# A smaller descriptor scratch, three more chunk places, and 17 chunks loaded ahead in the expert stage

## The chip, the cores and the metric

One core of one Trainium2 chip runs the program. The metric is the device time of one execution in microseconds. Three executions of the kernel before took 1064.9, 1062.97 and 1060.87 us; the median, 1062.97, is what the change is compared with.

## The reference

An encoder trunk of two layers works on 512 tokens of width 1024 in float32. Cut to what matters:

```python
h = layer_norm(x, ln0_g, ln0_b)
for i in range(DEPTH):
    u = h @ w_in[i]
    mix = concat([hyena(u), diff_attention(u), pool(u)]) @ w_out[i]
    h = layer_norm(DN_ALPHA * h + mix, ln1_g[i], ln1_b[i])
    y_moe = hier_moe(h, ...)     # top-1 group of 4, top-2 of its 4 experts; silu(h w1) * (h w3) @ w2
    y_ple = sigmoid(h @ ple_wg[i] + ple_bg[i]) * (p[i] @ ple_wp[i])
    h = layer_norm(DN_ALPHA * h + y_moe + y_ple, ln2_g[i], ln2_b[i])
return h
```

The kernel reads the weights of all 16 experts (three matrices of 1 MB each) from HBM once per layer.

## The kernel before, in words

All large weights come as a stream of units, 139 per layer. A unit is one chunk of weights (128 partitions of 4 KB, that is 512 KB) with the matmuls that use it. `pump` (from L233) handles the stream: SP issues the chunk's DMAs into a tile `raw` (L240), and `split` (L222 to L225) makes two tiles of it, `whi` by a cast on ACT (L224) and `wlo` by a subtraction on DVE (L225). PE then multiplies with three matmuls per product, hi by hi, hi by lo and lo by hi (`mm3`, L218 to L220). `pump` is called when a unit begins, with two depths: up to `ahead_raw` units further the loads are issued, and up to `ahead_split` units further the splits. The depths are pairs of numbers by stage, `P_A` (5, 3), `P_LN` (14, 1), `P_MOE` (14, 3, set in `layer` when the route is through), `P_END` (7, 3, from expert `E_END`, the tenth) and `P_LAST` (8, 4, in the last expert).

All tiles of 4 KB per partition are drawn from one pool by `s4` (L197): `raw`, `whi`, `wlo`, the stream `h`, the transposed tokens `xT`, the experts' outputs `ye`, the gate's `plz`, the attention's `prob` and so on. The pool has `NSLOT` places (L153), 33 before. A new tile waits for the last user of the tile whose place it takes; which that is comes out when the program is built. So the number of places and the depths together set which transfer, cast or subtraction waits for which.

The order of one layer: input projection, three head groups and output projection; LN1 (`gains` of LN1 are loaded at L293); the router (`route`), whose count `rt_cnt` is read by every engine at L1343 and decides at L1344 whether a rarely used branch for overfull experts is run; the gate's first half (`pl` matmuls, `plz`); 16 experts; LN2. SP's queue is in order, so a chunk that stands behind L1343 on SP is loaded when the count has come. An expert's tokens are gathered by an indirect DMA of POOL (`xe`, L1251), transposed, multiplied by w1 and w3 (four `in` units, two 256 KB DMAs each) and by w2 (two `out` units, 512 KB each), and scatter-added to `yd` in HBM by an indirect DMA of POOL (L1257). The place of `ye` comes free when that scatter has landed. The outputs of the last two experts are kept in `yl` and added at the end.

POOL's DMAs write their descriptors to a scratch in each partition's memory, whose size is an argument where the program is made (L1685). Outside the stages named, the order of instructions is the scheduler's, which sees a tile's wait for its place as any other wait.

Of the kernel before, what the change touches and what calls it, by code (L numbers as in the profile page):

```python
# [136 lines left out]
def _view(t, shape):  # L137
    if len(shape) == 2:
        return t
    letters = "abcdef"[:len(shape) - 1]  # L140
    return t.rearrange(f"p ({' '.join(letters)}) -> p {' '.join(letters)}", **dict(zip(letters, shape[1:])))
# [8 lines left out]


class Trunk:
    NSLOT = 33  # L153
    NHALF = 6
    FSTEPS = (0, 7), (1, 5), (3, 5), (3, 8)
    P_A = 5, 3
# [16 lines left out]
    P_LAST = 8, 4  # L173
    P_END = 7, 3
    P_LN = 14, 1
    P_MOE = 14, 3
    APART = [[], [0, 1, 3]]
    ZPE = [[1], [1, 2, 3]]

# [17 lines left out]
    def s4(self, shape, name, dt=F32):  # L197
        n = int(np.prod(shape[1:]))
        return _view(self.slots.tile([128, n], dt, name=name, tag="s4", bufs=self.NSLOT,
                                     padded_shape=[128, SLOT]), shape)  # L200
# [1308 lines left out]
    def layer(self, i):  # L1509
# [99 lines left out]
        self.xe, self.xT, self.act, self.actT, self.yl, self.hotT, self.plz = {}, {}, {}, {}, {}, {}, {}  # L1609
        self.ahead_raw, self.ahead_split = self.P_MOE  # L1610
        for e in range(2):
# [87 lines left out]
```

## Time and profile before

| | before |
|---|---|
| median of three executions | 1062.97 us (1060.87 to 1064.9) |
| the profiled execution | 1060.65 us, span 1058.7 us, mean granted clock 0.974 |
| PE busy | 977.4 us, 92% of the span |
| DVE, ACT, POOL busy | 779.3, 613.5, 166.3 us |
| DMA | 197.49 MB, mean 187 GB/s |

The span runs from the first to the last instruction; the profiled execution's own time is 2 us longer. "Busy" is time with an instruction in work; an engine that waits for a tile is idle, and the profile names the engine and line, or the DMA, whose end released it. `SPq` is SP's queue, which only issues DMAs here. Names as `raw<-in_moe_w_dram` are a DMA's target and source.

### The profile page before, as it was taken

The numbers are of one execution on the slowest core, as the hardware profiler recorded it, in microseconds if no ns is written. First come the engines' busy times: TensorE is split into PE (matmuls) and PEld (weight loads), VectorE is DVE, ScalarE is ACT, GpSimd is POOL, SyncE is SP. The second block draws the span as 40 slices with busy tenths as digits, with TensorE's granted clock in tenths as the row PEclk, the third lists the DMA queues.
The fourth block names the chain that finished last, engine by engine and source line by source line (L and its number), as shares of the span: only waits on it lengthen the run. The fifth ranks groups of instructions, "written<-read, shape, count | busy, mean of one in ns | idle before, by whom it ended". The sixth has DMA issues, their size and how long they took to land. (4 is left out here: it accounts for less than half of the span.)

```text
span 1058.7 us, 14409 instructions
## 1 busy us (share of the span) xinstructions
PE 977.4 (92%) x4869; PEld 805.7 (76%) x4870; DVE 779.3 (74%) x1301; ACT 613.5 (58%) x1046; POOL 166.3 (16%) x170
## 2 busy tenths in 40 slices
PE   4999999999889898999999999999998989999895
PEld 3887889897767676777768889798776768877673
DVE  7576887767685676878885578847678677888776
ACT  5425464656552746887754246654645375887673
POOL 1101000000122112332121100000002222333112
PEclk9999999999999998999989999999999999999998
DMA  8815121231864988999994412122186498899974
GB/s 261 234 35 140 51 79 42 70 95 65 308 209 109 334 245 274 292 300 308 264 312 122 112 55 66 49 64 88 50 307 221 107 329 275 283 311 318 306 211 159
DMA packets 156010, 197.49 MB, mean 187 GB/s; under 512 B 20296, under 2 KB 123786, under 8 KB 155925
## 3 DMA queue, kind: packets, MB, share of 16 engines
q1 hardware_dynamic: 135253, 155.58, 44.8%
q0 software_dynamic: 20672, 40.87, 15.1%
q8 instruction: 42, 0.69, 0.3%
q14 instruction: 43, 0.35, 0.1%
HBM read 182.85 MB, written 29.36 MB: 200 GB/s over the span
## 5 line engine op out<-in xcount | busy, mean ns | idle before, releaser
L225 DVE TENSOR_TENSOR wlo<-raw,whi 128x1024 fp32r<-128x1024 f32 (+2 forms) x278 | 321.9, 1182 | 78.9 <-ACT whi L224 68.1
L224 ACT CAST whi<-raw 128x1024 fp32r<-128x1024 f32 (+2 forms) x278 | 275.0, 1025 | 42.1 <-DMA yd<-ye,rt_tok 11.0
L218 PE MATMUL e<-whi,xT 128*128 128x512 f32 x256 | 108.8, 425 | 3.5 <-ACT xT L224 1.8
L219 PE MATMUL e<-wlo,xT 128*128 128x512 f32 x256 | 106.0, 414 | 5.9 <-DVE wlo L225 5.9
L220 PE MATMUL e<-whi,xT 128*128 128x512 f32 x256 | 103.4, 404 | 0.0
L218 PE MATMUL pj<-whi,hT 128*128 128x384 f32 x256 | 89.8, 351 | 2.3 <-ACT hT L224 1.8
L219 PE MATMUL pj<-wlo,hT 128*128 128x384 f32 x256 | 88.0, 344 | 0.3 <-DVE wlo L225 0.3
L220 PE MATMUL pj<-whi,hT 128*128 128x384 f32 x256 | 87.2, 341 | 0.2
L1257 POOL DMA_INDIRECT yd<-ye,rt_tok x28 | 47.0, 1677 | 196.5 <-ACT ye L1322 115.5
L868 ACT ACTIVATE prob<-sc,mx 128x512 f32<-128x512 f32 x64 | 43.7, 687 | 38.9 <-DVE mx L867 37.8
L219 PEld LDWEIGHTS e<-wlo,xT 128*128 128x128 f32 x256 | 50.0, 195 | 20.8 <-DVE wlo L225 12.0
L1251 POOL DMA_INDIRECT xe<-hd,rt_tok x32 | 48.2, 1507 | 100.4 <-PE tr L376 55.8
L218 PEld LDWEIGHTS e<-whi,xT 128*128 128x128 f32 x256 | 50.0, 195 | 14.5 <-ACT whi L224 3.5
L308 POOL TENSOR_TENSOR ors<-rs_y,mhalf 128x4 f32<-128x4 f32 x8 | 8.5, 1057 | 333.8 <-DVE rs_y L307 333.8
L220 PEld LDWEIGHTS e<-whi,xT 128*128 128x128 f32 x256 | 49.6, 194 | 10.2
L218 PE MATMUL mo<-whi,YT 128*128 128x512 f32 x128 | 53.6, 419 | 0.2 <-ACT YT L224 0.2
L219 PE MATMUL e<-wlo,actT 128*128 128x512 f32 x128 | 52.4, 409 | 1.2 <-DVE wlo L225 1.2
L218 PEld LDWEIGHTS pj<-whi,hT 128*128 128x128 f32 x256 | 48.7, 190 | 4.8 <-ACT hT L224 2.5
L218 PE MATMUL e<-whi,actT 128*128 128x512 f32 x128 | 48.5, 403 | 3.7 <-ACT whi L224 2.8
L219 PE MATMUL pl<-wlo,hT 128*128 128x512 f32 x128 | 51.3, 401 | 0.5 <-DVE wlo L225 0.5
L218 PE MATMUL pl<-whi,hT 128*128 128x512 f32 x128 | 51.1, 405 | 0.4 <-ACT whi L224 0.4
L220 PE MATMUL pl<-whi,hT 128*128 128x512 f32 x128 | 51.3, 401 | 0.0
(340 smaller groups left out, 2317.0 us busy)
## 6 DMA issues: line engine op xcount, KB each, us to landing
raw<-in_moe_w_dram SPq DMA_DIRECT2D x256, 256.0 KB
raw<-in_moe_w_dram SPq DMA_DIRECT2D x64, 512.0 KB
raw<-in_w_in_dram SPq DMA_DIRECT2D x96, 128.0 KB
raw<-in_w_in_dram SPq DMA_DIRECT2D x16, 512.0 KB
raw<-in_ple_wg_dram SPq DMA_DIRECT2D x16, 512.0 KB
raw<-in_w_out_dram SPq DMA_DIRECT2D x14, 512.0 KB
tabi<-c_tabi_dram POOLq DMA_DIRECT2D x8, 516.0 KB, 4.9
tabf<-c_tabf_dram POOLq DMA_DIRECT2D x8, 512.0 KB, 5.5
```

The lines of the kernel that those rows point to most:

```text
L218: mm(ps, a[0], b[0], start=start, stop=False)
L219: mm(ps, a[0], b[1], start=False, stop=False)
L220: mm(ps, a[1], b[0], start=False, stop=stop)
L224: self.nc.scalar.copy(hi, src)
L225: self.nc.vector.tensor_sub(lo, src, hi.bitcast(F32))
L308: nc.gpsimd.tensor_tensor(out, y, self.mhalf[:, :n], op=OP.pow)
L868: nc.scalar.activation(p[:, c], o, AF.Exp, bias=mx[:, c:c + 1], accum_out=sm[:, c:c + 1])
L1251: self.nc.gpsimd.indirect_dma_start(out=x, out_offset=None, in_=self.hd[:, :], in_offset=bass.IndirectOffsetOnAxis(ap=tok, axis=0), bounds ...
L1257: self.nc.gpsimd.indirect_dma_start(out=self.yd[:, :], out_offset=bass.IndirectOffsetOnAxis(ap=row, axis=0), in_=y, in_offset=None, bounds ...
```

## The change

Three numbers change: the scratch for descriptors is set to 4 KB per partition where it was the default of 16 KB; the 12 KB become three places of 4 KB in the pool; and the depth of loads in the expert stage is 17 where it was 14.

```diff
-    NSLOT = 33
+    NSLOT = 36
...
-    P_MOE = 14, 3
+    P_MOE = 17, 3
...
-    nc = _bacc.Bacc("TRN2", target_bir_lowering=False, num_devices=1)
+    nc = _bacc.Bacc("TRN2", target_bir_lowering=False, num_devices=1, dynamic_dma_scratch_size=4096)
```

On SP, in layer 0, this is the order around the read of the count before the change (a `raw` of 128x2x256 is half an `in` unit, one of 128x1024 an `out` unit; `gb` are the router's bias vectors):

```order
L1584 DMA bg<-in_ple_bg_dram 128x1024
L240 DMA raw<-in_moe_w_dram 128x1024 x2
L240 DMA raw<-in_moe_w_dram 128x2x256 x6
L1017 DMA gb<-in_moe_bgc_dram 128x4
L1017 DMA gb<-in_moe_bgf_dram 128x16
L1343 TENSOR_LOAD rt_cnt
L1343 ISA x2
L240 DMA raw<-in_moe_w_dram 128x2x256 x2
L1344 COMPARE_AND_BRANCH
```

And with the change:

```order
L1584 DMA bg<-in_ple_bg_dram 128x1024
L240 DMA raw<-in_moe_w_dram 128x1024 x2
L240 DMA raw<-in_moe_w_dram 128x2x256 x8
L240 DMA raw<-in_moe_w_dram 128x1024
L1017 DMA gb<-in_moe_bgc_dram 128x4
L1017 DMA gb<-in_moe_bgf_dram 128x16
L240 DMA raw<-in_moe_w_dram 128x1024
L1343 TENSOR_LOAD rt_cnt
L1343 ISA x2
L240 DMA raw<-in_moe_w_dram 128x2x256 x2
L1344 COMPARE_AND_BRANCH
```

One `in` unit and two `out` units more stand ahead of the read of the count; in layer 1 the same three units move ahead of it.

On DVE, in the last block of the attention of layer 0, the order changes as follows (`prob` is the softmax product of L873, `mx` its row maximum, `aT` the transposed probabilities, `mo` the output projection's sum):

```order
-L872 TENSOR_SCALAR rsm<-rsm,nlam,smx 128x1
-L225 TENSOR_TENSOR wlo<-raw,whi 128x1024
-L873 SCALAR_TENSOR_TENSOR prob<-prob,rsm 128x512
+L964 SCALAR_TENSOR_TENSOR h<-h,mo 128x512
+L871 RECIPROCAL rsm<-smx 128x1
+L964 SCALAR_TENSOR_TENSOR h<-h,mo 128x512
+L872 TENSOR_SCALAR rsm<-rsm,nlam,smx 128x1
+L225 TENSOR_TENSOR aT<-at,aT 128x4x128
+L873 SCALAR_TENSOR_TENSOR prob<-prob,rsm 128x512
+L225 TENSOR_TENSOR wlo<-raw,whi 128x1024
```

The subtraction `wlo` comes behind the last `prob`, and a subtraction `aT` ahead of it.

On PE, in the route of layer 0 (`lgT` are the router's scores, L1100 the counting of ranks; `pl` are the gate's matmuls that fill its gaps):

```order
 L218 MATMUL pl<-whi,hT_104 128x512
+L219 MATMUL pl<-wlo,hT_104 128x512
+L220 MATMUL pl<-whi,hT_105 128x512
+L218 MATMUL pl<-whi,hT_104 128x512
 L1032 MATMUL lgT<-hT_105,gwhl 20x256 x2
```

Three matmuls of the gate stand ahead of the scores, and in the same way four ahead of L1100. In the expert stage PE, DVE, ACT and POOL keep their order; there only SP's differs, by the three units and by the gains of LN2 (L293), which come three units later.

## Rows read from the trace of the kernel before

**Rows 1.** Page, part 1: busy time and share of the span, each engine.

```profile
span 1058.7 us, 14409 instructions
PE 977.4 (92%) x4869; PEld 805.7 (76%) x4870; DVE 779.3 (74%) x1301; ACT 613.5 (58%) x1046; POOL 166.3 (16%) x170
```

**Rows 2.** Table by stretches: start and end, length, busy time per engine, clock, DMA.

```profile
core 0: us, PE busy (x) PEld busy (x) DVE busy (x) ACT busy (x) POOL busy (x), PEclk, DMA share, GB/s
312.00:322.00 10.00, 10.00 (x55) 7.96 (x53) 8.93 (x41) 1.37 (x3) 0.00 (x0) 1.00 0.03 6
810.00:826.00 16.00, 15.52 (x89) 12.25 (x88) 14.34 (x48) 6.79 (x10) 0.00 (x0) 1.00 0.32 114
842.00:880.00 38.00, 35.16 (x162) 28.08 (x162) 30.40 (x36) 28.59 (x41) 12.32 (x8) 0.96 1.00 298
```

**Rows 3.** Waits of SP's queue: 312:340, 810:842, 880:913, 913:1000, in this order (us, times, longest).

```profile
SPq L1343 <- DVE rt_cnt L1131: 9.3, 1, 9.3
SPq L1343 <- DVE rt_cnt L1131: 16.7, 1, 16.7
SPq L240 <- DMA yd<-ye,rt_tok: 11.8, 2, 7.0
SPq L240 <- DMA raw<-in_moe_w_dram: 25.4, 43, 2.0
```

**Rows 4.** Timeline of ACT, 974:996: start, duration, operation, idle before and its releaser.

```profile
980.34 1.04 ACT L224 CAST whi<-raw 128x1024 fp32r<-128x1024 f32 x1 [3.32 <-DMA raw<-in_moe_w_dram]
```

**Rows 5.** Timeline of PE, 978:992.

```profile
981.44 0.50 PE L218 MATMUL e<-whi,actT 128*128 128x512 f32 x1 [1.24 <-ACT whi L224]
982.70 0.50 PE L219 MATMUL e<-wlo,actT 128*128 128x512 f32 x1 [0.76 <-DVE wlo L225]
987.86 0.73 PE L218 MATMUL pl<-whi,hT 128*128 128x512 f32 x2 [0.44 <-ACT whi L224]
989.12 0.50 PE L219 MATMUL pl<-wlo,hT 128*128 128x512 f32 x1 [0.53 <-DVE wlo L225]
```

**Rows 6.** Table by stretches, two short ones of the expert stages.

```profile
417.00:424.00 7.00, 6.81 (x23) 5.55 (x24) 5.10 (x6) 4.34 (x7) 1.59 (x1) 0.55 0.56 146
983.00:987.00 4.00, 4.00 (x11) 2.73 (x10) 2.40 (x4) 1.57 (x3) 0.00 (x0) 0.57 0.82 270
```

**Rows 7.** Timeline of PE, 1015:1030.

```profile
1022.74 0.50 PE L219 MATMUL e<-wlo,xT 128*128 128x512 f32 x1 [0.76 <-DVE wlo L225]
1025.70 0.50 PE L219 MATMUL e<-wlo,xT 128*128 128x512 f32 x1 [1.31 <-DVE wlo L225]
```

**Rows 8.** Waits of PE, 480:540.

```profile
PE e L219 <- DVE wlo L225: 2.1, 5, 0.8
PE el L1430 <- ACT yl L1315: 1.6, 1, 1.6
```

**Rows 9.** Timelines of DVE, 262:270, and PE, 264:272.

```profile
265.56 1.22 DVE L225 TENSOR_TENSOR wlo<-raw,whi 128x1024 fp32r<-128x1024 f32 x1
266.69 0.75 DVE L873 SCALAR_TENSOR_TENSOR prob<-prob,rsm 128x512 f32<-128x512 f32 x1
267.58 0.63 PE L881 MATMUL at<-cst,prob 128*128 128x128 f32 x4 [2.03 <-DVE prob L873]
```

**Rows 10.** Page, part 5: one group of the gate's matmuls.

```profile
L219 PE MATMUL pl<-wlo,hT 128*128 128x512 f32 x128 | 51.3, 401 | 0.5 <-DVE wlo L225 0.5
```

**Rows 11.** Tile ye, 330:1040: scatters; who waited for them; issue to landing.

```profile
L1257 POOL DMA_INDIRECT yd<-ye,rt_tok x28: 1575/1591/2011, 361.2 to 1025.1; - x28
  ACT whi L224: 11.0, 4
  DVE wlo L225: 4.7, 2
DMA to landing us min/median/max: 6.1/8.8/10.5
```

**Rows 12.** Timeline of PE, 412:428.

```profile
417.19 0.69 PE L1292 MATMUL e<-cst,act 128*128 128x128 f32 x2 [4.68 <-DVE act L1275]
```

## The prediction

> **What bounds the kernel now.** The page's first section comes first: TensorE (PE) is busy for 977.4 of 1058.7 us, and no other engine for more than 779.3 [rows 1]. So time can only be won where PE stands idle, 81 us in all, or runs at half clock, and the question is how much of this the three chunks reach. The table by stretches [rows 2] shows where DMA does not carry: while the router works the DMA engines are nearly empty, at a share of 0.03 (312 to 322 us, layer 0) and 0.32 (810 to 826, layer 1). Right behind it they are full, 1.00 at 298 GB/s in 842 to 880. In the expert stage the chunks come at what DMA gives, and a lead that was not laid up in the router's time can't be laid up later.
>
> Why DMA is empty there, the waits of SP's queue say [rows 3]: SP had issued all 14 chunks that its order allows and stood for 9.3 us (layer 0) and 16.7 us (layer 1) at L1343, where it reads the router's count. In 880 to 913 it waits 11.8 us for scatters, since the next chunk's place still holds a `ye` that is on its way out. In 913 to 1000 SP waits 43 times, 25.4 us, for its own earlier transfers: by then it is bandwidth and not places.
>
> What this comes to is on the timeline of ACT [rows 4]. At 980.34 the cast L224 starts after 3.32 us idle, released by the landing of its chunk: the lead of 14 chunks is used up. PE follows within 3 us [rows 5]: 1.24 + 0.76 + 0.44 + 0.53 = 2.97 us idle between 980 and 990, and behind the first gap the granted clock of 983 to 987 is 0.57 [rows 6], mostly the lower level of 1.2 GHz: 4 x 0.43 = 1.7 us more. The clock fell right behind the idle of 1.24 and 0.76 us, so I count it as a cost of these gaps. The starved stretch of layer 1 costs 4.7 us.
>
> **The change part by part.**
>
> *Three places more, 17 ahead.* As the orders of SP show, three more chunks (1.5 MB) stand ahead of L1343 in both layers, in time in which SP now waits. In 842 to 880 DMA moves 298 GB/s [rows 2], so three chunks of 524 KB are 1.57 MB / 298 = 5.3 us of DMA time, and the idle share offers 0.97 x 10 = 9.7 us in 312 to 322 and 0.68 x 16 = 10.9 us in 810 to 826: they fit. 5.3 us is thus the cap in each layer. The lead is not lost to the wait for scatters in 880 to 913: that wait ends when the scatter lands, and SP comes to it with three more chunks issued.
>
> Layer 1: the starved stretch goes, -4.7, under the cap. At the layer's end two more gaps of PE wait for `wlo`, 0.76 and 1.31 us [rows 7]; the second waits in truth for a place that a scatter holds, which three more places only hand to another tile. Ends 0 and -2.1, nearest -0.5, which I take.
>
> Layer 0: the same emptying shows as five waits of PE for `wlo` in 480 to 540, 2.1 us in all [rows 8]. They go: -2.1. The 1.6 us there for `yl` stay, as they hang on the expert's own result.
>
> *The depth falls back to 7 at expert 10 in both kernels.* From there a chunk's place comes from a few tiles back again, and SP pauses if it is further ahead than that. In 913 to 1000, in which expert 10 falls, SP waits mostly for its transfers [rows 3], that is, for DMA and not for a depth, so I charge 0. If it gives the lead back, rival 1 holds.
>
> *The attention tail of layer 0.* With other places free, one `wlo` subtraction now comes behind the softmax product L873 on DVE. Before, it ran 1.22 us right ahead of it, and PE waited 2.03 us for that `prob` [rows 9]. I take -1.0 (ends 0 and -1.2: no more than the subtraction itself).
>
> *LN1 and the route, both layers.* The fill matmuls of PE and the subtractions of DVE fall in other gaps of the router's chain; three or four `pl` matmuls, 401 ns each [rows 10], run ahead of a step of the chain instead of behind it: up to 1.6 us later or earlier for the count in each layer. PE has its fill work at either place, and is busy for 10.0 of 10 us in 312 to 322 [rows 2]. Taken as 0, kept as +-1.5 each.
>
> *Two vector loads of the router (L1017, layer 0) and the gains at expert 10* stand a few chunks later on SP; those small loads are for the next layer, and the gains are read when the layer ends. 0.
>
> *The scratch of 4 KB.* No row shows a scratch of another size. POOL, whose DMAs use it, is busy 16% [rows 1], and its scatters take 1591 ns to issue (median, maximum 2011) and land in 6.1 to 10.5 us [rows 11]. If nothing fills the smaller scratch, it costs 0. If each of the 28 scatters issued like the slowest, that is 28 x 0.42 = 11.8 us on an engine that is idle 84% of the time, under its cover; if that cover fails on one in ten, 1.2 us. I take 0 and keep +1.2 as the end. The Trainium skill (SBUF - State Buffer, "SBUF size: 192, 224, or 256?") calls the 16 KiB the carve-out of the descriptor ring and gives no smaller size; no run here shows one, and by it the sum would stay as it is while the ring does not fill.
>
> **Sum:** -4.7 - 0.5 - 2.1 - 1.0 = -8.3 us. The profiled execution took 1060.65 us; the median of the three runs is 1062.97, 2.3 above. On the median's footing: 1062.97 - 8.3 = **1054.7 us**.
>
> **The rivals.** What a measurement of this kernel can tell from no change is about 0.5%, 5.3 us: below 1057.7 is faster, above 1068.3 slower.
>
> 1. *The lead is given back.* Between the start of a stage and its starved stretch stand waits for scatters and, from expert 10, the depth of 7; if SP is stopped there by places or by order, both kernels reach 976 us with the same lead. For it: 11.8 us of scatter waits in 880 to 913, in which a lead is refilled in any case [rows 3]. Against it: in 913 to 1000 SP waits for its transfers. What is left is the attention tail and the end: 1062.97 - 1.5 = 1061.5, with the reordering of the route 1058 to 1065. Chance 0.27.
>
> 2. *A split waits for a scatter.* `whi` and `wlo` take places like any other tile, and where such a place held a `ye`, the cast waits for the scatter to land. Four casts and two subtractions did, 11.0 and 4.7 us [rows 11]. At 412 to 417 us one stood PE still for 4.68 us [rows 12], and 417 to 424 ran at clock 0.55 [rows 6], 7 x 0.45 = 3.2: 7.9 us for one event. The change deals out all places anew. It decides from the point where a cast's place is freed by a scatter that lands more than the lead of the splits (3 units, the 5.3 us of three chunks) after the cast could start. One new event cancels the gain (1062.6); two give 1062.97 - 8.3 + 15.8 = 1070.5. For it: all places move. Against it: only one of 28 scatters cost PE that much. Chance of one event 0.06 (within rival 1's band), of two 0.07.
>
> 3. *Scatters land later.* With more loads queued the scatters' 8.8 us could grow. The row against it is SP's wait for its own transfers [rows 3]: what is in flight is limited by that, not by the depth. The Trainium skill (DMA: Bandwidth & Descriptors, "Queues, rings and completion order") says that each DMA engine takes turns between queues packet by packet; by that rule a longer queue of SP would not delay a scatter, and the scatters' landings of 6.1 to 10.5 us beside a full DMA don't contradict it. The price without that: from +2 us of landing, each of the two scatter waits of 880 to 913 is 2 us longer and the gain halves: 1058.8. Chance 0.05.
>
> 4. *The scratch does stop POOL.* If an issue lasted until the DMA before it has landed, each scatter would hold POOL for some 8.8 us in place of 1.6 [rows 11]: 28 x 7.2 = 202 us, and with only a quarter of that in the way the time is past 1110. Only if a 4 KB scratch cannot hold one DMA. Chance 0.02.
>
> 5. *More than forecast.* Both layers give the whole cap of 5.3, the attention tail 1.2 and the route 1.5: 1062.97 - 13.3 = 1049.7. Chance 0.13.
>
> **How the numbers follow.** The forecast has 0.40, with its own range 1052 to 1058. Faster: rival 5 and nearly all of the forecast, a fifth of rival 1 and half of rival 3: 0.13 + 0.38 + 0.05 + 0.02 = 0.58. Slower: the two events, rival 4 and 0.02 for a bad order of the route on top of rival 1: 0.07 + 0.02 + 0.02 = 0.11. Within 0.5%: the rest, 0.31. The range leaves out about 0.1 on each side: from 1048.5 (rival 5 with a little more in the route) to 1064 (rival 1 with a bad route, or one event of rival 2).
>
> **What would show it.** Right: DMA share in the router's stretches of both layers up to about 0.5; no cast in layer 1 that waits over 1 us for a landing, no clock of 0.57 near 980; the waits for `wlo` in 480 to 540 below 1 us; POOL's issues at 1.6 us as before. Wrong: casts that still wait for landings at expert 11 or 12 with DMA full (the lead was given back); a PE gap over 2 us behind an ACT cast that a scatter released (rival 2); scatter landings with a median above 10 us (rival 3); POOL issues above 3 us (rival 4).

## The result and the profile after

The changed kernel takes 1050.84 us (median of four executions, 1046.77 to 1052.51) against 1061.97 us of the kernel before beside it. The ratio is 0.9878 with a 95% interval of [0.9845, 0.9911]: 13 us faster by the ratio and 11.1 by the two medians, where 8.3 were forecast. The profiled execution took 1046.77 us, its span is 1044.7 us, the granted clock 0.978.

To see where the time went, the start of the same matmul (same line, tile and count) is compared in two traces, after minus before, in us. `again` is the same changed kernel once more:

| point of the program | after | again |
|---|---|---|
| matmul `mo` ahead of the last attention block, layer 0 (253.9 before) | -2.7 | -1.9 |
| its last `at` transposes (267.6) | -3.8 | -3.0 |
| in the route, layer 0 (328.2) | -8.3 | -6.6 |
| a transpose of the second expert's tokens, layer 0 (340.2) | -7.6 | -6.3 |
| projection of layer 1, behind LN2 of layer 0 (562.8) | -12.3 | -13.3 |
| a transpose of the second expert's tokens, layer 1 (842.3) | -12.4 | -13.5 |
| middle of those experts (927.2) | -7.7 | -14.6 |
| ahead of the starved stretch (975.7) | -8.8 | -15.6 |
| behind it (987.9) | -13.5 | -20.4 |
| last expert (1025.7) | -16.0 | -22.8 |

Most of it was won before the experts of layer 1 began, and about half of that before any expert ran. The 1.9 and 2.7 us at the first line come from the program's start (1.7 and 1.1) and, in `after`, from a spell of half clock near 116 us that the kernel before had and `after` has not. They are of no meaning: `scratch_only` below, in the order of the kernel before, is at -1.5 there.

The timelines of DVE and PE in the last attention block of layer 0, after (start, duration, operation, idle before):

```profile
262.87 0.74 DVE L873 SCALAR_TENSOR_TENSOR prob<-prob,rsm 128x512 f32<-128x512 f32 x1
263.53 1.22 DVE L225 TENSOR_TENSOR wlo<-raw,whi 128x1024 fp32r<-128x1024 f32 x1
```

```profile
263.76 0.63 PE L881 MATMUL at<-cst,prob 128*128 128x128 f32 x4 [0.91 <-DVE prob L873]
```

`wlo` is behind `prob` now, and PE waits 0.91 us where it waited 2.03 [rows 9].

The router's scores of layer 0 on PE's timeline, first before, then after:

```profile
296.18 0.31 PE L1032 MATMUL lgT<-hT,gwhl 128*40 128x256 f32 x1 [2.31 <-ACT hT L224]
297.33 3.32 PE L1032 MATMUL lgT<-hT,gwhl 128*20 128x256 f32 x15 [0.85 <-DVE hT L225]
```

```profile
290.52 0.31 PE L1032 MATMUL lgT<-hT,gwhl 128*40 128x256 f32 x1 [0.24 <-ACT hT L224]
291.25 1.93 PE L1032 MATMUL lgT<-hT,gwhl 128*20 128x256 f32 x15 [0.42 <-DVE hT L225]
```

The gaps ahead of these scores shrink from 3.16 to 0.66 us. The `pl` matmuls are not the reason: the three that moved stand ahead of the second half's scores (300.94 us in `after`), where PE had no gap before either. The reason is on ACT and DVE, as in the attention tail. The scores need `hT`, a cast and a subtraction of the transposed tokens. Before, the split of one chunk stood just ahead of them, 1.03 us on ACT and 1.22 us on DVE:

```profile
294.13 1.03 ACT L224 CAST whi<-raw 128x1024 fp32r<-128x1024 f32 x1
295.54 1.07 ACT L224 CAST hT<-tr 128x512 fp32r<-128x512 f32 x2
...
295.46 1.22 DVE L225 TENSOR_TENSOR wlo<-raw,whi 128x1024 fp32r<-128x1024 f32 x1
296.60 1.28 DVE L225 TENSOR_TENSOR hT<-tr,hT 128x512 fp32r<-128x512 f32 x2
```

After, the split of the same chunk stands some 5 us ahead of them:

```profile
283.58 1.05 ACT L224 CAST whi<-raw 128x1024 fp32r<-128x1024 f32 x1
289.88 1.07 ACT L224 CAST hT<-tr 128x512 fp32r<-128x512 f32 x2 [0.18 <-PE tr L376]
...
284.66 1.23 DVE L225 TENSOR_TENSOR wlo<-raw,whi 128x1024 fp32r<-128x1024 f32 x1
290.50 1.29 DVE L225 TENSOR_TENSOR hT<-tr,hT 128x512 fp32r<-128x512 f32 x2
```

The 15 score matmuls took 3.32 us before and 1.93 now, at a clock that had fallen before and not now. The table by stretches has it for 296 to 302 us, first before, then after (columns as in rows 2):

```profile
296.00:302.00 6.00, 4.46 (x21) 3.14 (x22) 4.48 (x7) 2.22 (x5) 3.41 (x5) 0.72 0.65 203
```

```profile
296.00:302.00 6.00, 5.55 (x39) 4.60 (x38) 5.87 (x7) 4.55 (x8) 2.26 (x5) 1.00 0.80 253
```

That part is luck and not the change: in `again` the same matmuls ran at half clock behind the same short gap.

```profile
292.07 3.36 PE L1032 MATMUL lgT<-hT,gwhl 128*20 128x256 f32 x15 [0.41 <-DVE hT L225]
```

The table by stretches, after; the first two windows are those of [rows 2], moved to the same point of the program:

```profile
304.00:314.00 10.00, 9.61 (x43) 7.58 (x42) 8.29 (x36) 3.65 (x6) 0.00 (x0) 1.00 0.38 133
796.00:812.00 16.00, 15.58 (x83) 12.19 (x84) 13.48 (x47) 6.19 (x9) 0.00 (x0) 1.00 0.42 165
964.00:1000.00 36.00, 36.00 (x172) 29.23 (x171) 30.74 (x37) 27.57 (x40) 7.60 (x5) 1.00 1.01 294
```

The waits of SP's queue after, in the windows of [rows 3] moved in the same way (312 to 340, 790 to 842, 866.5 to 899.5, 899.5 to 987):

```profile
SPq L1343 <- DVE rt_cnt L1131: 10.3, 1, 10.3
...
SPq L1343 <- DVE rt_cnt L1131: 17.9, 1, 17.9
...
SPq L240 <- DMA yd<-ye,rt_tok: 13.3, 2, 6.7
...
SPq L240 <- DMA raw<-in_moe_w_dram: 20.2, 30, 2.1
```

DMA carries more in the router's time, 0.38 and 0.42 against 0.03 and 0.32 [rows 2], and SP still stands at the count, 10.3 and 17.9 us against 9.3 and 16.7 [rows 3]. In 964 to 1000 PE is busy for all 36.00 us, at full clock: the starved stretch [rows 4 to 6] is gone. SP's waits for scatters ahead of it are not: 13.3 us where 11.8 were (13.0 in `again`). Of layer 0's late subtractions in 470 to 530, one is left (PE's waits):

```profile
PE e L219 <- DVE wlo L225: 0.7, 1, 0.7
```

So far this is the forecast's picture. What it does not say is which of the change's numbers is needed for it, and there the forecast was wrong.

### The profile page after: what moved, and what is told of

It reads as the page before. It is cut to its first block, busy times and chain, and to the rows that moved or that the text cites. A ratio compares the mean times of both kernels' runs of the same rounds, so it can differ in the third digit from the quotient of the medians.

```text
span 1044.7 us, 14401 instructions
## 1 busy us (share of the span) xinstructions
PE 969.0 (93%) x4869; PEld 802.3 (77%) x4870; DVE 779.4 (75%) x1301; ACT 612.5 (59%) x1046; POOL 171.3 (16%) x170
## 5 line engine op out<-in xcount | busy, mean ns | idle before, releaser
L218 PE MATMUL pl<-whi,hT 128*128 128x512 f32 x128 | 51.0, 404 | 0.0
L219 PE MATMUL pj<-hT,whi 128*128 128x512 f32 x128 | 51.0, 399 | 0.0
L218 PE MATMUL pj<-hT,whi 128*128 128x512 f32 x128 | 51.0, 402 | 0.0
```

What stands on the lines that cost most here:

```text
L218: mm(ps, a[0], b[0], start=start, stop=False)
L219: mm(ps, a[0], b[1], start=False, stop=False)
```

## The experiments

The theory on record: three more chunks, loaded in the router's idle time, are a lead that carries the expert stage to its end. It needs the depth and the places together. The rivals: the places pay by themselves, or luck of the clock and of the scatters.

### The changed kernel again

No edit.

> The changed kernel once more, unaltered, for a second trace and a narrower ratio. Lead theory (three chunks more are loaded in the router's idle time and carry the expert stage): 10 to 13 us faster than before, and in the trace every cast of expert 11 to 15 in layer 1 starts with its chunk landed over 1 us earlier; no cast idle over 1 us for a landing between 960 and 1010 us. If the first trace's gain was luck of the clock and of scatters: 5 to 8 us faster, with the stretch of layer 1's LN1 to the count, or the starved stretch, as in the kernel before.

Measured: 1048.58 us (1042.45 to 1054.68), ratio 0.9878 [0.9829, 0.9928]. The gain stands. The two traces differ mostly by one event. In the first, a subtraction came late and PE waited 3.38 us for it; 911 to 917 then ran at half clock (PE's timeline and the table by stretches):

```profile
911.96 0.79 PE L219 MATMUL e<-wlo,xT 128*128 128x512 f32 x1 [3.38 <-DVE wlo L225]
```

```profile
911.00:917.00 6.00, 5.04 (x12) 3.87 (x13) 5.78 (x6) 1.53 (x2) 2.00 (x1) 0.50 1.02 351
```

The subtraction's place had held a `ye`: DVE stood from 905.69 to 910.64 us on the scatter that was issued at 900.33 and landed at 910.60 (the views name a cast of ACT that ended at the same time). `again` has no wait of PE in 900 to 920, and is 6.9 us ahead behind that place (-14.6 against -7.7 in the table above), 6.0 of them by this event. The same program has the event or not; one of them is about half of the 12 us by which executions of this kernel differ.

One sign of the lead theory held only in part: in `again` casts wait for landings from 970 us on, one of them 1.19 us.

### Places alone, and depth alone

`places_only`, against the changed kernel:

```diff
-    P_MOE = 17, 3
+    P_MOE = 14, 3
```

> 36 places with the depth of 14: SP issues the same chunks in the same order as before, so no chunk more is loaded ahead of the count. Lead theory: the attention tail (-1.0) and the new order around LN1 of layer 0 (-3.7 in the first trace) stay, the starved stretch near 980 us of layer 1 stays too (casts there wait over 1 us for landings): 4 to 6 us faster than before, about 1057. Rival (it is the places, through fewer waits for scatters, that pay): 9 us or more faster, about 1052, and no starved casts. Rival (only both together pay): 0 to 2 us faster.

Measured: 1047.77 us, ratio 0.9863 [0.9819, 0.9908]. All of the gain is there without one chunk more ahead of the count; the two intervals overlap.

`depth_only`, against the kernel before:

```diff
-    P_MOE = 14, 3
+    P_MOE = 17, 3
```

> Depth 17 with 33 places and the scratch of 16 KB: SP's order is that of the changed kernel, but the three chunks must wait for places that other tiles still hold. Lead theory: the three chunks find places late, the splits get places later as well; between 3 us faster and 4 us slower than before, 1059 to 1066. Rival (the depth is all, and places were free in the router's time): 7 us or more faster, about 1054.

Measured: 1073.24 us, ratio 1.011 [1.0061, 1.0159], 11.7 us slower than before: outside what either theory gave. So the gain does not need the depth: the places alone pay, and at 33 places the depth alone costs.

How the places do it, SP's waits show. Before, in 880 to 913, SP stood 11.8 us for scatters [rows 3]. In `places_only`, in 885 to 918, it waits for no scatter at all:

```profile
SPq L240 <- DMA raw<-in_moe_w_dram: 10.0, 18, 1.6
SPq L240 <- PE e L220: 2.3, 3, 1.3
SPq L240 <- PE e L219: 0.9, 1, 0.9
```

and its table by stretches has DMA at 0.97 in 880 to 913, and PE at full clock in 964 to 1000:

```profile
880.00:913.00 33.00, 30.99 (x148) 24.44 (x146) 25.15 (x30) 23.79 (x35) 7.98 (x6) 1.00 0.97 321
913.00:964.00 51.00, 49.69 (x234) 39.34 (x235) 44.38 (x53) 42.96 (x62) 15.80 (x10) 1.00 0.96 301
964.00:1000.00 36.00, 35.57 (x166) 28.54 (x165) 31.32 (x37) 26.23 (x36) 8.32 (x6) 1.00 1.00 302
```

The kernel before had in 880 to 913:

```profile
880.00:913.00 33.00, 33.00 (x156) 26.92 (x155) 25.24 (x29) 22.25 (x31) 6.35 (x4) 1.00 0.85 272
```

A difference of 0.12 over 33 us is 4 us of DMA time, two chunks. In the kernel before, the lead that was missing at 980 us was lost at places that scatters held; `places_only` does not lose it there.

The changed kernel does, and yet it is not starved. Why, a count of the lead shows: the chunks whose bytes have landed on SP's queue beyond the one that is being cast, from the traces' DMA packets. It is an estimate, good to about two chunks, since packets of several transfers are on their way at once. At four casts of layer 1, the same in each run (named by their times in the kernel before):

| cast | before | after | again | `places_only` | `depth_only` |
|---|---|---|---|---|---|
| 842.0, behind the count | 12 | 15 | 15 | 13 | 14 |
| 897.7 | 11 | 14 | 14 | 10 | 14 |
| 914.0 | 8 | 11 | 11 | 11 | 10 |
| 976.0, the last ahead of the starved stretch | 0 | 4 | 3 | 1 | 4 |

The three chunks more are there and last up to 976 us, in the changed kernel and in `depth_only`. `places_only` comes to the same place without them, since it loses none between 897.7 and 914.0. Either way leads past the stretch. Its price is not fixed either: `scratch_only`, in the order of the kernel before, passes it 2.8 us faster, at full clock and with 1.7 us of PE's waits in place of 2.97.

Over both expert stages (330 to 545 and 815 to 1040 us) SP waits for scatters for 38.3 us in the kernel before, 29.2 in `places_only`, 42.9 and 37.9 in the two traces of the changed kernel and 56.2 in `depth_only`. Casts and subtractions wait for them, by the tile's view, for 15.7, 7.2, 14.1 and 12.9, and 10.6 us. So the places alone take away a part of these waits, and with the depth of 17 most of it is back.

What depth 17 does at 33 places, ACT's and PE's timelines show at the worst spot (layer 1), and SP's waits in 913 to 1000:

```profile
880.78 1.04 ACT L224 CAST whi<-raw 128x1024 fp32r<-128x1024 f32 x1 [5.40 <-DMA yd<-ye,rt_tok]
```

```profile
883.47 0.69 PE L1292 MATMUL e<-cst,act 128*128 128x128 f32 x2 [4.33 <-DVE act L1275]
```

```profile
SPq L240 <- DMA yd<-ye,rt_tok: 21.2, 2, 14.1
```

A cast got the place of a `ye` and waited 5.40 us for its scatter; on ACT's queue the expert's activation stood behind it, DVE and PE behind that. With three chunks more in 33 places, fewer places go round for the casts, the subtractions and `ye`. SP waits 14.1 us at once for one scatter, and for 7.0 of them that scatter was not yet issued. These are the worst spots; that such waits make up all of the 11.7 us is not shown.

### The scratch alone

`scratch_only`, against the kernel before, and `scratch1k` with 1024 in its place:

```diff
-    nc = _bacc.Bacc("TRN2", target_bir_lowering=False, num_devices=1)
+    nc = _bacc.Bacc("TRN2", target_bir_lowering=False, num_devices=1, dynamic_dma_scratch_size=4096)
```

> Only the 4 KB scratch, 33 places and depth 14: the same instructions in the same order on every engine. Lead theory: no difference, within 2 us of before; POOL's scatters issue in 1.6 us and land in 6 to 10.5 us as before. Rival (the small scratch makes POOL wait): POOL issues above 3 us somewhere and 3 us or more slower.

Measured: ratio 1.0029 [0.9998, 1.0061], 1064.63 us. The interval just holds 1, so up to 0.6% can't be excluded. The scatters of its trace show nothing of it (compare [rows 11]):

```profile
L1257 POOL DMA_INDIRECT yd<-ye,rt_tok x28: 1575/1591/2452, 362.0 to 1030.4; - x28
...
DMA to landing us min/median/max: 7.9/8.9/9.9
```

> The kernel before with a scratch of 1 KB, a quarter of the change's; nothing else differs. scratch_only measured 1.0029 with an interval that just holds 1. If the size costs nothing: within 3 us of before, POOL's scatters at a median of 1.6 us and the eight table loads L504 at 0.76 us. If a scratch that fills costs: issues of the four table loads in a row (L504) and of the scatters grow to the landing of the DMA before, 4 us or more each, and the time is 5 us or more above before.

Measured: 1083.37 us, ratio 1.0179 [1.0144, 1.0215], 19 us slower: a scratch that is too small does cost, at a quarter of the change's size. That it costs by filling up is the likely reading, not a shown one. The issues themselves did not grow, which I had expected wrongly: POOL stands ahead of them, in time that no releaser explains (POOL's waits):

```profile
POOL yd L1228 <- issue: 24.4, 3, 9.9
POOL tabi L504 <- issue: 15.5, 4, 4.5
```

On its timeline the second of two gate transfers in a row, at L1228, is held for 9.91 us:

```profile
521.21 1.20 POOL L1228 DMA_DIRECT2D yd<-plz  x1 [9.91 <-issue]
```

The kernel before held it for 1.27 us, until its data was there:

```profile
507.41 1.19 POOL L1228 DMA_DIRECT2D yd<-plz  x1 [1.27 <-DVE plz L1208]
```

The waits at L504 cost nothing: the trace is within 0.2 us of the kernel before up to 340 us, and the loss comes in the expert stages, 11.8 us in layer 0 and some 6 in layer 1. With 4 KB there is no wait of this kind at L1228 or L504. (One wait of 8.3 us without a releaser stands in the changed kernel ahead of the last scatter of layer 0, but there the kernel before waits 8.1 us as well.) So 1 KB costs, and at 4 KB no cost could be measured.

### In which stage the places pay

`late36` has 36 places and depth 14, but three unused tiles hold three of them until the route of layer 0 is through; `early36` holds three from there to the end. The edits (`late36`; in `early36` the tiles are made where `late36` reads them, and read behind the last layer):

```diff
+        self.held = [self.s4([128, 1024], "held") for _ in range(3)]
+        for x in self.held:
+            nc.gpsimd.memset(x[:, :1], 0.0)
         self.setup()
...
         self.ahead_raw, self.ahead_split = self.P_MOE
+        if i == 0:
+            x = self.sm.tile([128, 4], F32, name="held_end", bufs=1)
+            for n, y in enumerate(self.held):
+                nc.gpsimd.tensor_tensor(x[:, n:n + 1], y[:, :1], self.gates[:, 0:1], op=OP.add)
```

> Depth 14 and 36 places, but three of them are held by unused tiles from the start until the route of layer 0 is through. The order of PE, DVE and SP is that of the kernel before up to there and behind it; only the places that tiles get in the expert stages (and in layer 1) differ. New theory (the places pay, in the expert stages through chunks and splits that wait less for scatters, and before them through another order in the attention tail and LN1 of layer 0): the expert part alone, 7 to 10 us faster than before, about 1054; the gap of 2.03 us ahead of the last prob of layer 0 stays. If nearly all comes from the new order ahead of the experts: 0 to 3 us faster.

Measured: 1055.58 us, ratio 0.9914 [0.9882, 0.9947], 9.1 us faster (0.0086 x 1063.4). The gap ahead of the last `prob` is 2.05 us, as before:

```profile
266.89 0.63 PE L881 MATMUL at<-cst,prob 128*128 128x128 f32 x4 [2.05 <-DVE prob L873]
```

> The complement: depth 14 and 36 places until the route of layer 0, then three places held by unused tiles until the program's end. New theory: only the new order ahead of the experts pays, 3 to 5 us faster than before, about 1058, and SP waits 10 us or more for scatters in 880 to 913 us or another stretch as long. If it is the expert stages alone that pay: 0 to 2 us faster. If the two parts don't add up (late36 and early36 together give more than 3 us less or more than places_only's 14.5), the waits of one stage shift the other.

Measured: ratio 0.997 [0.9941, 0.9999], 3.2 us faster. Its SP waits for scatters in 870 to 925, as in the kernel before:

```profile
SPq L240 <- DMA yd<-ye,rt_tok: 12.1, 2, 6.8
```

Both as the new theory said. 9.1 and 3.2 make 12.3; `places_only` gave 0.0137 x 1062.3 = 14.6, and the intervals cover the difference. About three quarters of the gain come from the stages behind the route of layer 0, and one quarter from the new order in its attention tail and LN1 (by the interval of `early36`, 0.1 to 6.3 us). Over both expert stages SP's waits for scatters are 29.1 us in `late36` and 34.6 in `early36`, those of casts and subtractions 8.9 and 17.0.

### Taking scatters out of the places

If waits for scatters are the cause, `ye` should have places of its own. `ye2_d14`, against `places_only` (`ye2_d17` and `ye2_d20` the same with 17 and 20 ahead):

```diff
-    NSLOT = 36
+    NSLOT = 34
...
-                    y = self.s4([128, 1024], "ye")
+                    y = self.slots.tile([128, 1024], F32, name="ye", tag="ye", bufs=2)
```

> The experts' outputs ye get two places of their own, 34 are left for all other tiles, depth 14: no chunk and no split can wait for a scatter any more. New theory: no cast, subtraction or load waits for a scatter; PE's gaps over 2 us in the expert stages, which all stand behind a split that waits for one, are gone; with 34 places at least as fast as the changed kernel, 1042 to 1050. Rival (it is the number of free places, whoever holds them): 34 are one third of the way, 5 us faster than before, about 1057. Rival (two places for ye are too few): ACT waits for scatters at L1322 over 2 us per expert and the time is above 1060.

> The same with depth 17. If the depth cost 11 us at 33 places only because splits then fell on places of ye: within 3 us of ye2_d14. If a depth beyond the places costs by itself (SP's order stops at a chunk without a place, the splits wait for places): 5 us or more above ye2_d14, with PE's gaps behind casts and subtractions that wait for other splits' places.

Measured: 0.9824 [0.979, 0.9858] and 0.9799 [0.9769, 0.9828], medians 1045.51 and 1042.55 us. Who waits for `ye` in `ye2_d17` (the tile's view; it is the whole list):

```profile
who waited for it (us, times):
  POOL yd L1257: 82.9, 14
```

No cast and no subtraction, and SP's waits in the two expert stages have no row for `ye` either. The changed kernel still has (same view):

```profile
  ACT whi L224: 10.7, 4
  DVE wlo L225: 3.4, 2
...
DMA to landing us min/median/max: 7.7/8.7/10.3
```

Not all gaps over 2 us of PE went, as I had said they would: in the expert stages `ye2_d14` keeps 2.26 and 3.00 us, `ye2_d17` 4.34 and 2.26. The two longest stand behind a cast that waits 2.18 and 3.02 us for `plz`, which leaves by such a transfer too. Nor is the time of `ye2_d14` clear of that of `places_only` (0.9863 [0.9819, 0.9908]), which shares as much memory.

> ye2_d17 with depth 20, which 34 places carry even less. If chunks waiting for places at the queue's head cost (as depth 17 at 33 places): 3 us or more above ye2_d17. If the depth is harmless once scatters hold no chunk's place: within 3 us of ye2_d17.

> 36 places that ye shares, depth 20. Where ye had its own two places, 14, 17 and 20 ahead gave 0.982, 0.980 and 0.976 of before; with shared places 14 and 17 gave 0.986 and 0.988. If the depth pays only where no scatter holds a place: no gain over 17, 0.985 to 0.997, with casts and subtractions that wait for scatters 8 us or more in all. If the depth pays either way: 0.982 or less.

Measured: `ye2_d20` 1037.68 us, 0.9762 [0.9728, 0.9796]: 25 us faster than the kernel before (0.0238 x 1063.8), and faster than the changed kernel, whose interval lies wholly above. It is also some 4 us faster than `ye2_d17`, better than either expectation, but there the intervals overlap. `depth20`, the changed kernel with 20 ahead and shared places, 1055.32 us, 0.9925 [0.9898, 0.9953]: no better than with 17. SP's waits of `depth20` in layer 0 (330 to 540):

```profile
SPq L240 <- DMA yd<-ye,rt_tok: 28.4, 5, 9.1
SPq L240 <- DVE wlo L225: 26.2, 13, 8.6
```

Its casts and subtractions wait only 8.4 us for scatters; it is the chunks that wait, and others behind them in SP's order. The changed kernel had 26.1 us of the first and 15.7 of the second row in layer 0, so most of what is new is the wait for subtractions. With places of their own for `ye`, going from 14 to 20 gives 0.6% more; with shared places it gives 0.6% back. Either step just clears its noise; the steps to 17 do not.

`ye2_31`: the memory of the kernel before, two places for `ye` and 31 for the rest.

```diff
-    NSLOT = 33
+    NSLOT = 31
...
-                    y = self.s4([128, 1024], "ye")
+                    y = self.slots.tile([128, 1024], F32, name="ye", tag="ye", bufs=2)
```

> No more memory than the kernel before: scratch of 16 KB, 33 places in all, but two of them kept for ye and 31 left for all other tiles, depth 14. If what counts is that chunks and splits don't wait for scatters: 3 to 10 us faster than before, no wait of SP, ACT or DVE for a scatter outside L1322. If the number of free places counts: at 31 chunks and splits wait for other tiles instead (PE and DVE releasers in SP's waits grow), and the time is 3 us or more above before.

Measured: ratio 1.0007 [0.9979, 1.0034], no difference. Between the two expectations: `ye` holds no place of the others any more, and the time is the same. So the number of places counts as well, and that the places pay by way of the scatters alone is not shown. The execution whose trace was kept took 1918.79 us, with PE busy almost twice as long as in any other (left out of the ratio), so the trace does not tell what waits there; that is open.

## Why the prediction was right, and where not

The direction and the range held (1050.84 within 1048.5 to 1064.0), and the forecast of -8.3 us came out as -13, within a factor of two. The argument held in parts only.

- **What bounds the kernel**: right. The time came from PE's gaps and the half clock behind them; PE's busy time over the span went from 92 to 93%.
- **Attention tail, -1.0**: right, 2.03 to 0.91 us, -1.1.
- **LN1 and the route, 0 +- 1.5**: mis-sized. In LN1 of layer 0 a split that no longer stands ahead of `hT` took 2.5 us of PE's gaps away (3.16 to 0.66), in both traces. I had seen that the subtractions of DVE fall in other gaps, but priced only the `pl` matmuls; for these it was right that PE has its fill work at either place. The row of 312 to 322 us on which I rested lies behind the scores, and PE's timeline at the scores I had not read. The 1.4 us more of the first trace (3.32 to 1.93 us for the 15 score matmuls) were luck of the clock, as `again` shows. `early36` puts tail and LN1 together at 3.2 us.
- **Starved stretch of layer 1, -4.7**: right in size, as 975.7 to 987.9 gives -4.7 in the table of the result (-4.8 in `again`), and right in its mechanism for the changed kernel, which comes there with 3 to 4 chunks where the kernel before had none. Both kernels lose three chunks to the waits for scatters, so that a lead "is not lost" to them held as well. The step that failed is "a lead that was not laid up in the router's time can't be laid up later". `places_only` lays up nothing more in the router's time and wins the same stretch (-12.1 to -16.2 at the same matmuls), since it does not lose chunks at places that scatters held. So the stretch is no proof of the depth, and -4.7 was as much the price of the places.
- **End of layer 1, -0.5**: too small. From 987.9 to 1025.7 the table gives -2.5 and -2.4, more than the end of -2.1.
- **Layer 0, -2.1**: PE's waits for `wlo` went from 2.1 to 0.7 us. But more was won: layer 0's experts gave 4.7 us in `after` and 7.0 in `again` (from 340.2 to 562.8), in part since the event at 412 to 417 [rows 12] shrank, from 4.68 us of gap to 3.13 and 3.31. The term was too small by more than half.
- **The scratch, 0**: within what could be measured; 1.0029 leaves up to 0.6% open. Something like rival 4 appears at 1 KB, at 19 us.
- **Rival 2** was rated as an odd event. One such event came, in the first trace of the changed kernel, of 6.0 us (-13.7 at 915 us to -7.7 at 927), where 7.9 was the price. The waits behind it are common: 15.7 us of casts and subtractions in the kernel before, 14.1 and 12.9 in the changed one, 7.2 in `places_only`. How much of the gain goes by them is open, since `ye2_31` takes `ye` out of the shared places at 33 and gains nothing.
- **Rival 1** (the lead is given back) did not happen, as the count at 976 us shows. But its time for a change without that lead, 1061.5, was far off too: `places_only` has none of it and takes 1047.77 us. I treated depth and places as one edit, and gave the places no term of their own.
- **Rival 3** fell: scatters land in 8.7 us at the median, 8.8 before [rows 11], and 8.8 in `depth20`. The rule of the Trainium skill (DMA: Bandwidth & Descriptors, "Queues, rings and completion order"), by which engines take turns between queues, agrees.

## What to carry to other kernels

When loads, working tiles and slow outgoing transfers share one pool of places, ask of every new place and of every step of depth which tile's place it hands to whom: a place that a scatter holds for 9 us stops a queue that works in order, and everything behind it. Places of their own for the tiles that leave by a slow transfer gave nothing that could be measured by themselves (`ye2_31`, and `ye2_d14` beside `places_only`), but with them more depth paid: from 14 to 20 ahead, 0.6% faster apart and 0.6% slower shared. Test the numbers of an edit one at a time, since a forecast can be right in time and wrong in cause.

## What was not expected of the hardware

A descriptor scratch of 1 KB made POOL stand 24.4 us ahead of three transfers of L1228 and 15.5 us ahead of four of L504, in stretches of up to 9.9 us, about as long as a transfer of L1228 takes to land (8.8 us at the median in that run), and cost 1.8%. At 4 KB no trace shows such a stretch at these lines. The Trainium skill (SBUF - State Buffer, "SBUF size: 192, 224, or 256?") counts 16 KiB for it; the changed kernel runs with a quarter of that.
